# Multi-query attention on one core: the cube of a pair of units as one product, VectorE's units from the second on, planner settings by a table

## The chip, the core and the metric

The kernel runs on one core of a Trainium2 chip. Five engines of the core matter here. TensorE (PE in the profile; PEld is its weight load) multiplies matrices and writes to PSUM. ScalarE (ACT) evaluates the exponential. VectorE (DVE) and GpSimd (POOL) do elementwise work, GpSimd on SBUF alone. SyncE (SP) issues DMAs. Each engine runs its own instructions in order, and semaphores order them between engines. The metric is the device time of one execution in microseconds; smaller is better. The kernel before was timed three times: 744.91 us is the median, 744.78 and 746.61 the ends.

## The reference

Eight batches, 1,024 positions, 16 query heads of 64 numbers, one key and value head per batch:

```python
scores = np.matmul(q, k.transpose(0, 1, 3, 2)) / np.sqrt(head_dim)
weights = np.exp(scores - np.max(scores, axis=-1, keepdims=True))
weights = weights / np.sum(weights, axis=-1, keepdims=True)
attn_out = np.matmul(weights, v)
```

q, k, v and the output are fp32. The result is q's shape, (8, 1024, 16, 64).

## The kernel before

**Units.** Two heads are done together. For a pair of heads, a half of 512 queries and a tile of 128 keys the kernel makes one *unit*: `scores` (L279) multiplies the transposed keys by the transposed queries, one matmul of 512 columns for each head, and leaves 128 x 1,024 scores in PSUM. There are 8 batches x 8 head pairs x 2 halves x 8 key tiles = 1,024 units, 2,048 such matmuls. Three PSUM slots (`sc0` to `sc2`) hold units that wait to be exponentiated.

**Two ways to an exponential.** Most units go to ScalarE, which makes one ACTIVATE of 1,024 columns (`scalar_exp`, L292) into a tile `wt`. The others (called V units) go to VectorE. There `ve_bits` (L303) reads PSUM and writes the scores as int16 bits of an fp16 number. Two V units make a *pair* (`PAIR = 2`), and the next passes run on both at once, 2,048 columns: `ve_mantissa` (L316), `ve_power` (L326) and `ve_square` (L337). The last step is the *cube*, a product of the mantissa's number with its square. It is dealt between GpSimd (`ve_cube`, L345) and VectorE (`ve_rest`, L353): GpSimd takes some columns while VectorE does something that reads PSUM, VectorE takes what is left. Here a cube belongs to one unit and has 1,024 columns, since `cube_of` gives the columns of that unit alone. For a pair in the set `two`, `ve_shift` (L341) follows the square, and its units need two terms instead of three below.

**Values.** `value` (L420) multiplies the exponentials by the values: for each of 16 head pairs and halves of a batch (each is one `h` of the planner), 8 groups of 128 queries of one head, and in each group one matmul of 65 columns for each *term*. A ScalarE unit is one term, a V unit three (two in the set `two`): the power, the bits and the cube. All terms of a group must be there before its sum is complete; the order is first all units' own terms, then the powers, then the cubes. Seven groups fill a PSUM bank, which VectorE inverts and scales (`inverse` L370, `finish` L379) into `osb`; SyncE stores it.

**The order of the work** is written out ahead by `plan()`, a planner that runs on the host. It advances a modelled time of each engine with fixed costs (`T_MM`, `T_ACT`, `VE_COST`, `GP_COL` and others) and emits operations. At each step it decides whether TensorE does scores (`issue`) or values, which units go to VectorE (`wants`), what VectorE does next (`vector_step`), and how many columns GpSimd gets (`share`). A stretch of scores between two stretches of values is called a *round* here; it holds the scores of one or more units. What settles these choices are constants: `REST`, `DEFER`, `HOLD`, `VE_SLACK`, `RATE`, `SAFE` and others, the same for the whole run. `SAFE` (300 ns) is added to the time at which a value's input is ready in the model. `wants` allows V units from unit `NKT` (8) to unit `STEPS - V_END`. The queue of GpSimd also issues the loads of q and v, in `share`, right behind a cube.

**The start.** q of the first head pair arrives in fp32 (`qf`, two DMAs on ScalarE's queue). ScalarE casts the first half to fp16 (L868), VectorE the second (L875). TensorE transposes them (`first_q`, L232), and ScalarE or VectorE copies the result to `qt` (L245). Keys go the same way (`first_k`, L216 and L228). After unit 1 the second half of q is turned.

**The end.** The last `h` has its own 64 value matmuls (`last_values`), behind them reciprocals, a check of the sums and the last stores.

Of the kernel before, what the change touches and what calls it, by code (L numbers as in the profile page):

```python
# [26 lines left out]
TWO_N = 1  # L27
TWO_M = 16
LONE = 12
# [35 lines left out]
NEXT = {"bits": 0.0, "inverse": 0.0, "finish": 60.0}  # L65
MINC = 128
REST = 896
LATE = 0.0
EPS = 0.0
AWAY = 500.0  # L70
SLACK1 = -500.0
SOON = 0.0
FIRST = 90.0
DEFER = 12
HOLD = 1400.0
VE_SLACK = 1800.0
V_END = 16
RATE = 0.25
NEAR = 200.0
WAIT = 50.0  # L80
T_BITS = 1255.0
SAFE = 300.0
# [3 lines left out]
def attention_main(ctx, tc, q, k, v, out, flag):  # L86
# [46 lines left out]
        w3p.tile([P, PAIR, 3, 2, QCH], FP16, tag=f"w3_{N_W3 - 1}", name="qf")  # L133
        .rearrange("p n i h q -> p (n i h q)")[:, 0 : 2 * NKT * P]
# [33 lines left out]
    def load_q_first(p):  # L168
        x = wtp.tile([P, 2, QCH], FP16, tag=f"wt{N_WT - 1 - p}", name=f"q16_first{p}")
        q16[("first", p)] = x.rearrange("p h (c f) -> p (h c) f", f=P)  # L170
        src = q[0, :, 2 * p : 2 * p + 2, :].rearrange("(c p) h d -> p c (h d)", p=P)
        if p:
            nc.gpsimd.dma_start(out=q16[("first", p)], in_=src)
# [67 lines left out]
    def first_q_out(ps, p, cs, eng):  # L241
# [3 lines left out]
        eng(out=qt[0][:, p, at], in_=ps[:, at])  # L245
# [66 lines left out]
    def parts(u, n, i):  # L312
        return ve[u][:, 0:n, i]
# [37 lines left out]
    def ve_rest(u, lo):  # L351
        we, wu = cube_of(u)
        return nc.vector.tensor_tensor(  # L353
            out=wu[:, lo:], in0=we[:, lo:], in1=wu[:, lo:], op=ALU.mult
# [10 lines left out]
    def cube_of(u):  # L365
        return (ve[u, 0][:, i].rearrange("p h q -> p (h q)") for i in (1, 2))
# [124 lines left out]
    def plan():  # L491
# [5 lines left out]
        t_pe = t_ve = t_act = t_gp = t_now = 0.0  # L497
        mode = "v"
        u = 0
        free = [0.0] * 3  # L500
# [9 lines left out]
        members = {}  # L510
        lead = {}
# [32 lines left out]
        def cost(what, v):  # L544
            return VE_COST[what, 2] if (what, 2) in VE_COST and len(members[v]) == 2 else VE_COST[what]
# [5 lines left out]

        def share(s):
# [4 lines left out]
            v = next((v for v in left if left[v]), None)  # L557
            if v is not None:
# [3 lines left out]
                if n >= MINC:  # L562
                    lo = 2 * QCH - left[v]
                    emit(gs, "cube", v, lo, lo + n, gate)
                    left[v] -= n
                    lock = gs + GP_FIX + n * GP_COL
                    t_gp = lock + GP_TAIL
                    ready[v, 2] = max(ready.get((v, "g"), 0.0), t_gp)
                    ready[v, "g"] = ready.pop((v, 2))
# [6 lines left out]
        def passes(v):  # L576
            nonlocal half, made_2
            chain.extend([("mantissa", v), ("power", v), ("square", v)])
            half = None
            made_2 += 1  # L580
            if made_2 * TWO_N % TWO_M < TWO_N:
                chain.append(("shift", v))
                two.update(members[v])

        def vector_step(limit):

            nonlocal t_ve, t_gp, lock, behind, t_behind, early, last, half
            if half is not None and not todo and (flush or u - half > LONE or min(wt_used) == float("inf")):
# [3 lines left out]
            for x in [(r, "bits", v, 0) for v, r in todo] + evict:  # L592
                r, what = x[:2]
                s = max(t_ve, r, min(w3_used) if what == "bits" and half is None else 0.0)
                key = (max(s, t_ve + NEXT[what]), ORDER[what], x[2])
# [3 lines left out]
                best[1] <= t_ve + NEXT[best[2][1]]  # L599
                and (best[2][1] == "bits" or behind is not None or best[2][0] < t_ve - LATE or not chain)  # L600
            )
            if urgent and best[2][1] == "bits" and not any(left.values()):
                t = 0.0
                for what, v in chain:
                    t += cost(what, v)
                    if what == "square":
                        urgent = t > HOLD
                        break
            if not urgent and (
                chain or left and (flush or left[next(iter(left))] <= REST or u - next(iter(left)) > DEFER)  # L610
# [422 lines left out]
```

## Time and profile before

| | us |
|---|---|
| median of three runs | 744.91 |
| profiled execution | 745.27 |
| its span, first to last instruction | 743.3 |
| first score matmul starts | 6.33 |
| first ACTIVATE of line 292 starts | 6.98 |
| last ACTIVATE ends | 737.0 |
| the 64 last value matmuls start | 735.66 |

| engine | busy us | share of the span | instructions |
|---|---|---|---|
| TensorE matmul | 728.4 | 98% | 13,826 |
| TensorE weight load | 490.5 | 66% | 13,826 |
| ScalarE | 732.0 | 98% | 798 |
| VectorE | 713.0 | 96% | 1,139 |
| GpSimd | 362.4 | 49% | 306 |

Matmuls and ScalarE's operations overlap, so a busy share near 100% does not tell by itself which engine sets the pace; the starts of neighbouring instructions and the waits do. In a line of the timeline the columns are start, length, engine, line, operation, and in brackets the idle time before it with what ended it.

### The profile page before, as it was taken

Reading aid. Unit: us, or ns where it says so; the run is one execution under the profiler, and the core shown is the slowest. Engines: PE = TensorE matmul, PEld = TensorE weight load, DVE = VectorE, ACT = ScalarE, POOL = GpSimd, SP = SyncE. Lnnn points to the kernel's source line nnn. Section 1 sums busy time; section 2 is a strip of 40 time slices with the busy share of each in tenths; the row PEclk is TensorE's granted clock in tenths of the full one; section 3 lists DMA queues with packets and bytes.
Section 4 is the critical chain, followed back from the end, with each engine's and each line's share of the span. In section 5 each row is a group of like instructions: output and inputs, shape, how many; then the busy total and the mean of one; then the engine's idle time right before and its main releaser. Section 6 shows DMA issues by size and latency. Waiting matters only on the chain.

```text
span 743.3 us, 31083 instructions
## 1 busy us (share of the span) xinstructions
PE 728.4 (98%) x13826; PEld 490.5 (66%) x13826; DVE 713.0 (96%) x1139; ACT 732.0 (98%) x798; POOL 362.4 (49%) x306
## 2 busy tenths in 40 slices
PE   6999999999999999999999999999999999999997
PEld 3566666666666666666666666666666666666675
DVE  3999999999999999999999999999999999999994
ACT  7999999999999999999999999999999999999996
POOL 3555454554455554445454445554554544554540
PEclk9999999999999999999999999999999999999999
DMA  9986547665385654686358654365525765212112
GB/s 188 167 102 116 80 86 119 113 109 106 63 108 120 110 88 86 87 138 108 81 101 123 116 108 81 79 125 107 115 69 92 108 130 101 60 45 60 44 52 82
DMA packets 168921, 73.87 MB, mean 99 GB/s; under 512 B 94032, under 2 KB 161616, under 8 KB 168784
## 3 DMA queue, kind: packets, MB, share of 16 engines
q1 hardware_dynamic: 149152, 53.76, 34.8%
q0 software_dynamic: 18576, 17.57, 19.5%
q8 instruction: 109, 1.79, 1.0%
q10 hardware_dynamic: 1056, 0.52, 0.2%
q14 instruction: 28, 0.23, 0.1%
HBM read 37.75 MB, written 33.55 MB: 96 GB/s over the span
## 4 chain that ended last, share of the span: by engine, by line
PE 78%; ACT 15%; DVE 5%; issue 1%; DMA 0%; DVEq 0%; ACTq 0%
PE ot L420 46%; PE sc L279 32%; ACT wt L292 15%; DVE we L303 2%; DVE osb L379 1%; DVE we L337 1%; DMA knat<-in_k_dram 0%; DVE we L316 0%; DVE we L326 0%; DVE we L353 0%; PE kps L216 0%; DVE rec_all L370 0%; DVE ge L460 0%; DVE both L466 0%; DVE ok_all L470 0%
## 5 line engine op out<-in xcount | busy, mean ns | idle before, releaser
L292 ACT ACTIVATE wt<-sc 128x1024 f16<-128x1024 f32 x795 | 729.6, 1205 | 1.2 <-PE sc L279 1.1
L345 POOL TENSOR_TENSOR we<-we 128x832 f16<-128x832 f16 (+15 forms) x223 | 314.8, 1412 | 361.4 <-DVE we L337 225.6
L420 PE MATMUL ot<-vp,wt 128*128 128x65 f16 x6296 | 424.8, 194 | 0.2 <-ACT wt L292 0.2
L420 PE MATMUL ot<-vp,we 128*128 128x65 f16 x5384 | 416.7, 194 | 0.0
L420 PEld LDWEIGHTS <-wt 128*128 128x128 f16 x6296 | 314.5, 97 | 93.6 <-issue 93.2
L420 PEld LDWEIGHTS <-we 128*128 128x128 f16 x5384 | 310.7, 97 | 81.6 <-issue 79.8
L279 PE MATMUL sc<-qt,k2t 64*128 64x512 f16 x2048 | 341.4, 385 | 4.9 <-ACT wt L292 3.7
L303 DVE TENSOR_SCALAR we<-sc 128x1024 int16<-128x1024 f32 x229 | 278.4, 1216 | 8.0 <-PE sc L279 6.6
L279 PEld LDWEIGHTS <-k2t 64*128 64x128 f16 x2048 | 95.3, 93 | 66.0 <-issue 9.8
L337 DVE TENSOR_TENSOR we<-we 128x2048 f16<-128x2048 f16 (+1 forms) x115 | 138.2, 1202 | 0.0
L379 DVE TENSOR_TENSOR osb<-ot,rec_all 128x448 f32<-128x448 f32 x146 | 89.2, 611 | 0.4
L353 DVE TENSOR_TENSOR we<-we 128x512 f16<-128x512 f16 (+13 forms) x222 | 83.4, 377 | 0.0
L316 DVE TENSOR_SCALAR we<-we 128x2048 int16<-128x2048 int16 (+1 forms) x115 | 78.5, 682 | 0.3
L326 DVE TENSOR_SCALAR we<-we 128x2048 int16<-128x2048 int16 (+1 forms) x115 | 77.9, 678 | 0.0
L182 POOL DMA_DIRECT2D q<-in_q_dram x64 | 41.3, 648 | 2.0 <-DMA q_first<-in_q_dram 1.4
L370 DVE RECIPROCAL rec_all<-ot 128x7 f32<-128x7 f32 x146 | 28.5, 195 | 7.3 <-PE ot L420 7.3
L164 POOL DMA_DIRECT2D vp<-in_v_dram x8 | 7.3, 907 | 0.0
L216 PE MATMUL kps<-ident,k 128*64 128x128 f16 x16 | 1.3, 314 | 4.3 <-DVE k L207 4.2
L250 DVE TENSOR_SCALAR k16d<-knat 128x1024 f16<-128x1024 f32 x7 | 4.8, 682 | 0.0
L341 DVE TENSOR_SCALAR we<-we 128x2048 f16<-128x2048 f16 x7 | 4.7, 667 | 0.1
L245 DVE COPY qt<-qps 128x512 f16<-128x512 f16 (+1 forms) x2 | 1.1, 555 | 3.5 <-PE qps L232 3.5
L216 PEld LDWEIGHTS <-k 128*64 128x64 f16 x16 | 0.8, 159 | 4.6 <-DVE k L207 4.6
(31 smaller groups left out, 23.3 us busy)
## 6 DMA issues: line engine op xcount, KB each, us to landing
out_dram<-osb SPq DMA_DIRECT2D x109, 256.0 KB, 2.5
q<-in_q_dram POOLq DMA_DIRECT2D x56, 256.0 KB, 4.7
out_dram<-osb SPq DMA_DIRECT2D x38, 128.0 KB, 2.3
knat<-in_k_dram SPq DMA_DIRECT2D x7, 256.0 KB, 4.2
q<-in_q_dram POOLq DMA_DIRECT2D x8, 192.0 KB, 7.4
vp<-in_v_dram POOLq DMA_DIRECT2D x8, 128.0 KB, 6.4
qt<-q SPq DMA_TRANSPOSE x64, 4.9
qf<-in_q_dram ACTq DMA_DIRECT2D x2, 256.0 KB, 3.9
```

Source lines behind the costliest of these rows:

```text
L182: nc.gpsimd.dma_start(out=q16[(b, c)], in_=q[b, c * P : (c + 1) * P, h0:, :].rearrange("p h d -> p (h d)"),)
L279: nc.tensor.matmul(sc[u][:, hh, :], k2t[r : r + 64, j * P : (j + 1) * P], qt[b][r : r + 64, p % HP, c * QCH : (c + 1) * QCH], start=True, ...
L292: nc.scalar.activation(out=w, in_=sc.pop(u), func=EXP, scale=escale, bias=math.log(CS))
L303: return nc.vector.tensor_scalar(out=w3[:, 1].bitcast(I16), in0=sc.pop(u), scalar1=15.0 * 1024, scalar2=0.0, op0=ALU.add, op1=ALU.max,)
L316: return nc.vector.tensor_scalar(out=parts(u, n, 2).bitcast(I16), in0=parts(u, n, 1).bitcast(I16), scalar1=0x3FF, scalar2=0x3800, op0=ALU. ...
L326: return nc.vector.tensor_scalar(out=parts(u, n, 0).bitcast(I16), in0=parts(u, n, 1).bitcast(I16), scalar1=0x7C00, scalar2=0x0201, op0=ALU ...
L337: return nc.vector.tensor_tensor(out=m, in0=m, in1=m, op=ALU.mult)
L345: x = nc.gpsimd.tensor_tensor(out=wu[:, lo:hi], in0=we[:, lo:hi], in1=wu[:, lo:hi], op=ALU.mult)
L353: return nc.vector.tensor_tensor(out=wu[:, lo:], in0=we[:, lo:], in1=wu[:, lo:], op=ALU.mult)
L370: return nc.vector.reciprocal(out=rec_all[:, g0 : g0 + n], in_=o[:, 0:n, D])
L379: x = nc.vector.tensor_tensor(out=ob[:, i0 : i0 + n, :], in0=o[:, 0:n, 0:D], in1=rec.unsqueeze(2).broadcast_to([P, n, D]), op=ALU.mult,)
L420: nc.tensor.matmul(ots[g0][:, gg - g0, 0 : D + 1], w[:, hh, qb * P : (qb + 1) * P], kv[h // (HP * NCH)]["vp"][:, ci, u % NKT, 0 : D + 1], ...
```

## The change

- **Layout.** A pair's tile is `[P, 3, PAIR, 2, QCH]` instead of `[P, PAIR, 3, 2, QCH]`: each of the three parts (power, bits, mantissa) is now 2,048 neighbouring columns over both units.
- **Cube.** `cube_of` gives these 2,048 columns, so a cube and its rest belong to a pair and may cross from one unit to the other; `ve_rest` gets an upper bound. In the planner `left`, `squared` and `group` are kept by pair, and `cubed` notes for each unit when its last column is done.
- **V units** may begin with unit 1 (`V_START`) and reach to unit `STEPS - 12`. The planner counts VectorE and GpSimd as occupied for the first 2.5 and 2.6 us (`T_VE0`, `T_GP0`).
- **Settings by table.** 11 sets of 19 settings (`WAYS`), of which a letter of `TABLE` picks one for each stretch of 32 units. `safe`, which was 300 everywhere, is 0 in 10 of the 32 stretches, 150 in 7 and 300 in 15. `rate` is 1.0 (0.25 before), `rest` 640 to 1,536 (896), `defer` 16 or 20 (12). The choice of pairs with a shift is by a rule on VectorE's backlog (`two`) instead of every sixteenth pair.
- **Start.** q of the first head pair is transposed in fp32 straight from `qf` (`first_qf`); the two casts are gone. The first half goes through two score slots, two tiles each, copied by ScalarE and VectorE with 256 columns each. The second half of the keys is turned after unit 0, the second half of q after unit 1, and `prep_v` comes after unit 3.

Counted in the two built programs, in their order:

| | before | after |
|---|---|---|
| ACTIVATE of a unit | 795 | 792 |
| V units / pairs, singles among them | 229 / 115 | 232 / 116 |
| shift passes | 7 | 6 |
| value matmuls without the last 64 | 11,680 | 11,744 |
| rounds of one unit / two units | 311 / 349 | 279 / 365 |
| rounds of 3 / 6 / 9 units | 3 / 1 / 0 | 0 / 1 / 1 |
| GpSimd cubes, columns in all | 223, 138,688 | 149, 160,128 |
| VectorE rests, columns in all | 222, 95,808 | 113, 77,440 |
| loads of q, of v; stores; transposes by DMA | 64, 8; 147; 71 | the same |

```diff
-V_END = 16
-RATE = 0.25
-SAFE = 300.0
+V_END = 12
+V_START = 1
+Way = namedtuple(
+    "Way",
+    "slack wait near bits end late least rest defer hold rate safe away alone eps soon first lone two",
+)
+SPAN = 32
+TABLE = (
+    "feekajaddbabacdckibcabadbddfahag"
+)
+WAYS = (
+    Way(1500.0, 100.0, 200.0, 0.0, 60.0, 1500.0, 96, 640, 16, 350.0, 1.0, 300.0, 500.0, -500.0, 0.0, 0.0, 90.0, 16, -1.0),
+    Way(1800.0, 200.0, 2000.0, 0.0, 60.0, 2500.0, 96, 896, 16, 1400.0, 1.0, 0.0, 500.0, -200.0, 50.0, 0.0, 90.0, 8, -1.0),
...
+)
+T_VE0 = 2500.0
+T_GP0 = 2600.0
...
+    def first_qf(ps, cs):
+        for c in cs:
+            nc.tensor.matmul(
+                ps[:, (c - cs[0]) * P : (c - cs[0] + 1) * P],
+                qf[:, c, :],
+                ident,
+                is_transpose=True,
+                start=True,
+                stop=True,
+            )
...
-            ve[u] = w3p.tile([P, PAIR, 3, 2, QCH], FP16, tag=f"w3_{i}", name=f"we{p}_{c}_{j}")
-            ve[u, 0] = ve[u][:, 0]
-        else:
-            ve[u, 0] = ve[first][:, 1]
-        w3 = ve[u, 0]
+            ve[u] = w3p.tile([P, 3, PAIR, 2, QCH], FP16, tag=f"w3_{i}", name=f"we{p}_{c}_{j}")
+        w3 = ve[first][:, :, int(first != u)]
...
-        return (ve[u, 0][:, i].rearrange("p h q -> p (h q)") for i in (1, 2))
+        return (ve[u][:, i].rearrange("p n h q -> p (n h q)") for i in (1, 2))
...
+        def cubed(v, n, t):
+
+            lo = 2 * QCH * len(group[v]) - left[v]
+            left[v] -= n
+            for k, x in enumerate(group[v]):
+                if lo < (k + 1) * 2 * QCH <= lo + n:
+                    ready[x, 2] = t
...
-                NKT <= u < STEPS - V_END
+                V_START <= u < STEPS - V_END
...
-                and made_v < (u - NKT + 1) * RATE
+                and made_v < (u - V_START + 1) * way.rate
...
                 if r < float("inf"):
-                    r += SAFE
+                    r += way.safe
...
+        if u == 0:
+            first_k(kps, 1)
+            first_k_out(kps, 1)
+        if u == 3:
+            prep_v(0)
         if u == 1:
-            first_q(turned[0], 0, range(NKT // 2, NKT))
-            first_q_out(turned[0], 0, range(NKT // 2, NKT), nc.vector.tensor_copy)
+            turned[0] = bank("qps0")
+            first_qf(turned[0], range(NKT // 2, NKT))
+            first_q_out(turned[0], 0, range(NKT // 2, NKT), nc.vector.tensor_copy, NKT // 2)
...
-        nc.scalar.copy(out=q0[:, 0 : NKT // 2, :], in_=qf[:, 0 : NKT // 2, :])
         first_k(kps, 0)
-        first_q(turned[0], 0, lo)
-        first_q_out(turned[0], 0, lo, nc.scalar.copy)
+        ps = [scp.tile([P, 2, QCH], FP32, tag=f"sc{i + 1}", name=f"qps0_{i}")[:, 0] for i in range(2)]
+        for i in range(2):
+            first_qf(ps[i], range(2 * i, 2 * i + 2))
+        first_q_out(ps[0], 0, range(0, 2), nc.scalar.copy, 0)
         first_k_out(kps, 0)
-        first_k(kps, 1)
-        first_k_out(kps, 1)
-        nc.vector.tensor_copy(out=q0[:, NKT // 2 :, :], in_=qf[:, NKT // 2 :, :])
-        prep_v(0)
+        first_q_out(ps[1], 0, range(2, 4), nc.vector.tensor_copy, 2)
```

More of the change, by code (lines that the diff above doesn't have):

```diff
@@ L556, in share @@
                 return
-            v = next((v for v in left if left[v]), None)
+            v = next(iter(left), None)
             if v is not None:
@@ L605, in vector_step @@
                     t += cost(what, v)
-                    if what == "square":
-                        urgent = t > HOLD
+                    if what == ("shift" if v in two else "square"):
+                        urgent = t > way.hold
                         break
             if not urgent and (
-                chain or left and (flush or left[next(iter(left))] <= REST or u - next(iter(left)) > DEFER)
+                chain or left and (flush or left[next(iter(left))] <= way.rest or u - next(iter(left)) > way.defer)
             ):
```

133 lines of the change are left out of this document (66 added, 67 removed).

## The prediction

> **What bounds the kernel now.** I read the table of windows first, then TensorE's waits, then the timeline around one round, then the chain and the groups. Windows (busy us of PE, PEld, DVE, ACT and POOL, then granted clock and DMA):
>
> ```profile
> 6.33:28.00 21.67, 18.18 (x198) 9.03 (x197) 14.57 (x21) 20.65 (x23) 5.71 (x12) 0.92 1.19 180
> 100.00:200.00 100.00, 100.00 (x1903) 67.73 (x1902) 99.19 (x156) 100.00 (x110) 52.34 (x43) 1.00 0.57 97
> 200.00:225.00 25.00, 24.20 (x472) 16.16 (x471) 24.90 (x40) 25.00 (x28) 11.27 (x10) 1.00 0.79 116
> 350.00:600.00 250.00, 249.70 (x4780) 168.30 (x4776) 247.34 (x394) 250.00 (x274) 127.11 (x103) 1.00 0.55 102
> ```
>
> TensorE, ScalarE and VectorE are all full, GpSimd half. The chain of work that ended last and TensorE's waits tell them apart:
>
> ```profile
> PE 78%; ACT 15%; DVE 5%; issue 1%; DMA 0%; DVEq 0%; ACTq 0%
> ...
> PE sc L279 <- ACT wt L292: 3.7, 10, 0.5
> PE sc L279 <- DVE we L303: 1.0, 3, 0.6
> ```
>
> In 743 us TensorE waits under 5 us for a score slot, and hardly for a value's input. So its own work is the bound, once it is fed. What that work costs is read in the timeline of weight loads:
>
> ```profile
> 404.17 0.13 PEld L420 LDWEIGHTS <-we 128*128 128x128 f16 x2
> 404.35 0.10 PEld L279 LDWEIGHTS <-k2t 64*128 64x128 f16 x2
> 404.68 0.15 PEld L420 LDWEIGHTS <-wt 128*128 128x128 f16 x3 [0.23 <-issue]
> ...
> 730.26 0.10 PEld L420 LDWEIGHTS <-wt 128*128 128x128 f16 x1
> 730.40 0.32 PEld L279 LDWEIGHTS <-k2t 64*128 64x128 f16 x4
> 730.95 0.10 PEld L420 LDWEIGHTS <-wt 128*128 128x128 f16 x1 [0.23 <-issue]
> ...
> 733.01 0.97 PEld L420 LDWEIGHTS <-wt 128*128 128x128 f16 x30
> ```
>
> Values follow each other at (0.97 - 0.10) / 29 = 0.030 us; over all stretches of the timeline the mean is 0.0295. From the last value before a round of one unit to the first behind it is 0.48 us (404.20 to 404.68), the median of all such 0.473; for two units 0.69 (730.26 to 730.95), the median 0.690. Less the value's own step, a round of one unit costs 0.4435 and one of two 0.6605: the second unit in a round adds only 0.217. With the counts of the program, before is 11,680 x 0.0295 = 344.6, plus 311 x 0.4435 = 137.9, plus 349 x 0.6605 = 230.5, plus the four longer rounds 4.1: **717.1 us of work**. It begins at 6.33, and the last 64 values begin at 735.66, so TensorE was idle 735.66 - 6.33 - 717.1 = 12.2 us. Summing the same prices along the timeline puts 9.3 us of this before 28 us and 2.9 after it. Check: 6.33 + 717.1 + 12.2 + 7.64 (tail to 743.3) + 1.97 (743.3 to 745.27) = 745.24.
>
> **Part by part: TensorE's work.** 64 more values: +1.9. 32 fewer rounds of one unit, -14.2; 16 more of two, +10.6; three of three (0.8775 each) go, -2.6; the round of 9, +2.2. After: 346.4 + 123.7 + 241.1 + 3.7 = 714.9, **-2.2 us**. All of it is on the path. ScalarE has 3 units fewer at 0.904 (the commonest distance of two ACTIVATE starts), -2.7, no separate gain.
>
> **The start.** The chain to the first score is here:
>
> ```profile
> 4.21 0.64 PE L216 MATMUL kps<-ident,k 128*64 128x128 f16 x8 [4.21 <-DVE k L207]
> 4.38 0.62 ACT L868 CAST q_first<-qf 128x512 f16<-128x512 f32 x1 [1.20 <-DMA qf<-in_q_dram]
> 5.05 0.61 PE L232 MATMUL qps<-ident,q_first 128*128 128x128 f16 x4 [0.20 <-ACT q_first L868]
> 5.70 0.58 ACT L245 COPY qt<-qps 128x512 f16<-128x512 f16 x1 [0.70 <-PE qps L232]
> 6.33 1.04 PE L279 MATMUL sc<-qt,k2t 64*128 64x512 f16 x4
> 8.54 0.29 DVE L267 TENSOR_SCALAR vp<-vp 128x512 f16<-128x512 f16 x1 [1.36 <-DMA vp<-in_v_dram]
> ```
>
> The ACT cast goes (0.62), and the copy is halved between two engines. The four transposes are fp32 now, and the trace has none of that. Lower bound: the fp16 row, 0.61 for four. Upper bound: the score matmul of four times the columns, 0.385 each in the groups, 1.54 for four. They start at 4.65, behind the keys' issue. VectorE's copy of the keys (4.89 to 5.31) and its 256 columns of q (0.25) follow: first score at 5.6 to 6.6. I take 6.1, the middle, for neither row is near: -0.2. [...]
>
> What follows decides more. Unit 1 goes to VectorE, but its bits stand behind `prep_v`, which waits for v's DMA (8.54 before), so they start at 8.8; if q's second half is late, 10.3. Behind them up to the first pair's rest stand five bits (1.13), a copy of q (0.65), two each of mantissa and power (0.60) and square (1.14), one rest (0.6): 11.6 us. The cube is whole at 20.4 to 22, and TensorE can't pass the first group of half 0 before that. By then its work is 18 units and 12 values, 6.2 us, so its idle time is 8.2 to 9.4. From there it has a half's 96 values at hand, and the next pair's cube is about 5.3 us of VectorE work behind, 26 us. I take 9.3 as before; bounds 8.3 and 11.3. The second unit of ScalarE comes behind eight key transposes, score 1 and four fp32 ones, 0.3 to 1.5 us after it is free: inside the same idle time, since TensorE lacks the cube anyway.
>
> **VectorE and GpSimd.** Groups and VectorE's timeline:
>
> ```profile
> L353 DVE TENSOR_TENSOR we<-we 128x1024 f16<-128x1024 f16 x14 | 9.5, 678 | 0.0
> L353 DVE TENSOR_TENSOR we<-we 128x192 f16<-128x192 f16 x36 | 8.8, 245 | 0.0
> ...
> L345 POOL TENSOR_TENSOR we<-we 128x512 f16<-128x512 f16 x65 | 75.3, 1159 | 162.2 <-DVE we L337 100.0 <-PE sc L279 35.6 <-PE ot L420 19.5
> L345 POOL TENSOR_TENSOR we<-we 128x1024 f16<-128x1024 f16 x4 | 8.8, 2207 | 13.7 <-DVE we L337 6.7 <-DVE rec_all L370 3.5 <-DVE we L341 3.4
> ```
>
> A rest costs 0.52 ns a column (433 ns for 832 columns) and some 0.065 us besides, its overlap with the next taken off: 64.2 before, 113 x 0.065 + 77,440 x 0.00052 = 47.6 after, -16.6. Three bits, one pair's passes and one shift less add 5.1: VectorE is 11.5 us lighter. GpSimd gains 21,440 columns at about 2.05 ns and loses 74 starts of 0.11: some +36 of 315 us, under its 381 idle. Loads of q and v stand behind its cubes, now one in 5 us instead of 3.3; their transposes come 20 units (14 us) later, and landing took 4.7, so that wait stays hidden, with SyncE's stores behind it.
>
> VectorE is not the bound, so its relief pays only where it was late: idle 2.9 after 28 us, the largest piece in 200 to 225, where three check operations (214.84 to 216.43) delay bits and TensorE waits 0.55 and 0.25 for them. I take 0.5 of the 2.9, 0 and 2.9 being the ends of this gain.
>
> A long cube can also cost VectorE: in the timeline a cube ends in the median 0.06 us after the next pass on SBUF has started, and rests of 512 columns beside cubes lasted 427 ns where the line through 192 and 1,024 columns gives 412. I leave it at that, since there are fewer cubes. [...]
>
> **Sum:** 6.1 + 714.9 + 9.3 + 2.4 + 7.64 + 1.97 = 742.3 against 745.27. The profiled execution lies 0.36 above the median of the runs, so 742.0 beside 744.91.
>
> **Rivals.** (1) The gain is eaten. (1a) At the start: fp32 transposes at the upper end and a late first cube, idle 11.3 instead of 9.3: 744.5. For it: nothing feeds TensorE but that one cube. Against: before idles as long. [...] (2) Slower: TensorE meets cubes that aren't done. `safe` is 0 in 10 of 32 stretches, 40 halves of units. A wait for GpSimd in a value was 0.9 us in three times, 0.3 each. At 0.3 a half it is 12 us, 754; at half of that 748. It equals the gain at 0.07 us a half, and is slower by 0.3% at 0.13. Against: only three such waits before. (3) The lighter VectorE takes away all 2.9 of the later idle time and the start its 1 us: 738.6 to 740.
>
> **Numbers.** Forecast 0.50, its own range 740.6 to 743.6; (1a) 0.14, (1b) 0.08; (2) 0.16; (3) 0.12. 0.3% of 744.91 is 2.2 us, about what a measurement can tell from no change: 742.7 and 747.1. Faster: four fifths of the forecast, all of (3), a little of (1) and (2): 0.56. Slower: half of (2): 0.08. Same: 0.36. The range of 739.6 to 746.2 leaves out the lower half of (3) and the upper half of (2) and little else.
>
> **What would show it.** Right: first score at 5.6 to 6.6, 20 to 22 us for the first group's end, TensorE idle 9 to 10 by 28 us and under 3 after, 792 ACTIVATEs back to back. [...]

## The result and the profile after

The changed kernel takes 747.9 us, the median of 22 runs (746.9 to 748.6). The kernel before, run beside it as often, takes 746.11 (744.78 to 747.5). The ratio is 1.0026, with a 95% interval of 1.0019 to 1.0033: **slower by a quarter of a per cent**. That is inside the 0.3% called "no change" ahead, but the interval excludes 1, the sign is opposite to the forecast, and 747.9 lies above the range of 739.6 to 746.2. The 744.91 shown ahead was the median of three runs; of the 22, nine lie under 745.0 and eleven over 746.2. The median of such a set jumps, so kernels are compared below by their ratios to runs of the kernel before made beside them.

The profiled execution took 747.03 and has a span of 745.3 (before: 745.27 and 743.3). With the prices of the prediction (0.0295 a value, 0.4435 a round of one unit, 0.6605 a round of two) summed along each trace, the span falls into five parts. What is left over at such a price counts as idle, so a matmul at half clock leaves its excess there.

| us | before | after | difference |
|---|---|---|---|
| first score starts | 6.33 | 6.40 | +0.1 |
| TensorE's work by prices | 716.7 | 714.5 | -2.2 |
| TensorE idle up to 28 us | 9.3 | 12.5 | +3.2 |
| TensorE idle later | 3.3 | 4.1 | +0.8 |
| tail behind the last 64 values' start | 7.64 | 7.76 | +0.1 |
| span | 743.3 | 745.3 | +2.0 |

The loss is in the first 28 us. The table of windows of the changed kernel (busy us of PE, PEld, DVE, ACT, POOL, then granted clock, DMA share and GB/s) shows it in its first row:

```profile
6.40:28.00 21.60, 16.27 (x136) 7.25 (x138) 16.91 (x21) 17.78 (x19) 9.45 (x13) 0.84 1.20 189
100.00:200.00 100.00, 99.77 (x1932) 66.94 (x1932) 98.84 (x141) 99.75 (x110) 51.28 (x28) 1.00 0.48 98
200.00:225.00 25.00, 25.00 (x492) 17.01 (x488) 24.57 (x37) 25.00 (x29) 14.85 (x8) 1.00 0.63 119
350.00:600.00 250.00, 249.70 (x4826) 170.33 (x4826) 245.93 (x355) 249.66 (x273) 136.31 (x74) 1.00 0.55 101
```

In mid-run TensorE is as full as before, and does more matmuls in the same time (4,826 against 4,780 in the last row, whose counterpart stands in the prediction). In the first row it does 136 where the kernel before does 198, ScalarE is busy 17.78 us instead of 20.65, and the granted clock is 0.84 instead of 0.92. Two things happen there. The first is in the timeline behind the first score (start, length, engine, line, operation):

```profile
4.77 1.12 PE L249 MATMUL qps<-ident,qf 128*128 128x128 f32 x4
...
6.40 0.61 PE L296 MATMUL sc<-qt,k2t 64*128 64x512 f16 x2 [0.52 <-DVE qt L262]
...
6.94 0.64 PE L222 MATMUL kps<-ident,k 128*64 128x128 f16 x8
7.05 1.02 ACT L309 ACTIVATE wt<-sc 128x1024 f16<-128x1024 f32 x1 [1.19 <-PE sc L296]
7.51 0.61 PE L296 MATMUL sc<-qt,k2t 64*128 64x512 f16 x2
...
8.05 1.11 PE L249 MATMUL qps<-ident,qf 128*128 128x128 f32 x4
...
9.10 1.04 PE L296 MATMUL sc<-qt,k2t 64*128 64x512 f16 x4
...
9.74 2.85 ACT L309 ACTIVATE wt<-sc 128x1024 f16<-128x1024 f32 x3 [1.67 <-PE sc L296]
...
10.02 1.21 DVE L317 TENSOR_SCALAR we<-sc 128x1024 int16<-128x1024 f32 x1
```

Between the first unit and ScalarE's second stand eight key transposes, the score of unit 1 (VectorE's) and four fp32 transposes of q. ScalarE is free at 8.07 and starts at 9.74; before, its second ACTIVATE started at 7.90. VectorE's first bits start at 10.02, though their score was done by 8.12 (7.51 + 0.61): VectorE's queue has other work ahead of them, shown at late_turns below.

The second is the granted clock. The same view in smaller windows, of the kernel before and then of the changed one:

```profile
14.00:20.00 6.00, 5.23 (x84) 3.14 (x81) 4.72 (x6) 6.00 (x8) 0.00 (x0) 1.00 1.33 174
20.00:24.00 4.00, 2.97 (x18) 1.07 (x17) 4.00 (x7) 4.00 (x5) 2.65 (x3) 0.92 0.87 155
24.00:28.00 4.00, 4.00 (x61) 2.55 (x60) 3.77 (x5) 3.63 (x5) 1.45 (x2) 0.65 1.04 180
```

```profile
14.00:20.00 6.00, 3.50 (x25) 1.20 (x22) 5.97 (x8) 5.51 (x7) 1.90 (x2) 1.00 1.14 197
20.00:24.00 4.00, 2.70 (x19) 0.80 (x17) 3.88 (x5) 3.62 (x5) 3.62 (x3) 0.57 1.07 128
24.00:28.00 4.00, 4.00 (x58) 2.49 (x57) 2.88 (x4) 3.36 (x4) 2.34 (x2) 0.58 1.22 237
```

From 14 to 20 us TensorE does 25 matmuls instead of 84, since with VectorE's units in the first half it has hardly a group to finish without a cube. Then the clock falls to 0.50 for 6.83 us (20.57 to 27.39), against 3.41 us before (23.35 to 26.77). Just then the first cube becomes whole, and TensorE has values to do. GpSimd's last piece and VectorE's rest of that cube, in the timeline:

```profile
20.36 2.11 POOL L359 TENSOR_TENSOR we<-we 128x544 f16<-128x544 f16 x1 [0.58 <-DVE we L340]
...
22.45 0.66 DVE L367 TENSOR_TENSOR we<-we 128x992 f16<-128x992 f16 x1
```

It is whole at 23.11 (22.45 + 0.66), where the prediction said 20.4 to 22.

### The profile page after: what moved, and what is told of

Read it like the earlier page. It is cut to its first block, busy times and chain, and to the rows that moved or that the text cites. A ratio compares the mean times of both kernels' runs of the same rounds, so it can differ in the third digit from the quotient of the medians.

```text
span 745.3 us, 31135 instructions
## 1 busy us (share of the span) xinstructions
PE 729.1 (98%) x13890; PEld 490.6 (66%) x13890; DVE 712.2 (96%) x1035; ACT 729.7 (98%) x794; POOL 399.4 (54%) x232
## 4 chain that ended last, share of the span: by engine, by line
PE 87%; DVE 9%; ACT 2%; issue 1%; DMA 1%; DVEq 0%
PE ot L434 51%; PE sc L296 35%; DVE we L317 4%; ACT wt L309 2%; DVE we L351 1%; DVE osb L393 1%; DVE we L340 1%; DVE we L330 1%; DMA out_dram<-osb 0%; DMA knat<-in_k_dram 0%; DVE we L367 0%; PE qps L249 0%; PE last L457 0%; DVE rec_all L384 0%; PE kps L222 0%
## 5 line engine op out<-in xcount | busy, mean ns | idle before, releaser
L359 POOL TENSOR_TENSOR we<-we 128x1472 f16<-128x1472 f16 (+19 forms) x149 | 348.7, 2341 | 327.7 <-DVE we L351 188.8
L434 PE MATMUL ot<-vp,we 128*128 128x65 f16 x5472 | 421.1, 194 | 0.0
L434 PEld LDWEIGHTS <-we 128*128 128x128 f16 x5472 | 317.3, 98 | 92.4 <-issue 91.2
L317 DVE TENSOR_SCALAR we<-sc 128x1024 int16<-128x1024 f32 x232 | 282.1, 1216 | 12.5 <-PE sc L296 11.5
L351 DVE TENSOR_TENSOR we<-we 128x2048 f16<-128x2048 f16 x116 | 139.3, 1201 | 0.0
L296 PEld LDWEIGHTS <-k2t 64*128 64x128 f16 x2048 | 93.4, 93 | 65.1 <-issue 13.2
L330 DVE TENSOR_SCALAR we<-we 128x2048 int16<-128x2048 int16 x116 | 81.9, 706 | 1.5
L340 DVE TENSOR_SCALAR we<-we 128x2048 int16<-128x2048 int16 x116 | 79.5, 685 | 0.0
L367 DVE TENSOR_TENSOR we<-we 128x544 f16<-128x544 f16 (+22 forms) x113 | 57.8, 511 | 0.0
L188 POOL DMA_DIRECT2D q<-in_q_dram x64 | 43.4, 681 | 2.0 <-DMA vp<-in_v_dram 1.1
```

The costliest lines, as they stand in the source:

```text
L188: nc.gpsimd.dma_start(out=q16[(b, c)], in_=q[b, c * P : (c + 1) * P, h0:, :].rearrange("p h d -> p (h d)"),)
L296: nc.tensor.matmul(sc[u][:, hh, :], k2t[r : r + 64, j * P : (j + 1) * P], qt[b][r : r + 64, p % HP, c * QCH : (c + 1) * QCH], start=True, ...
L317: return nc.vector.tensor_scalar(out=w3[:, 1].bitcast(I16), in0=sc.pop(u), scalar1=15.0 * 1024, scalar2=0.0, op0=ALU.add, op1=ALU.max,)
L330: return nc.vector.tensor_scalar(out=parts(u, n, 2).bitcast(I16), in0=parts(u, n, 1).bitcast(I16), scalar1=0x3FF, scalar2=0x3800, op0=ALU. ...
L340: return nc.vector.tensor_scalar(out=parts(u, n, 0).bitcast(I16), in0=parts(u, n, 1).bitcast(I16), scalar1=0x7C00, scalar2=0x0201, op0=ALU ...
L351: return nc.vector.tensor_tensor(out=m, in0=m, in1=m, op=ALU.mult)
```

## The experiments

Three theories for the 3.2 us at the start. **A, turns:** the transposes of keys and q between the first scores ("turns") delay the second ACTIVATE and VectorE's first bits, and with them everything behind. **B, clock:** the scarce work lets the granted clock fall, and the values run at half speed. **C, early units of VectorE:** with VectorE's units from unit 1 on, TensorE lacks work until the first cube. Rivals in mid-run: long cubes, late cubes. One table for all runs; times and ratios beside it. "Half clock" is the length of the stretches at 0.50 before 40 us. The columns of work, idle time, half clock and ACTIVATEs come from one profiled execution of each kernel, the ratios from all its runs.

| kernel | TensorE's work | idle to 28 us | idle later | half clock | 1st, 2nd ACTIVATE | median, us | ratio to before |
|---|---|---|---|---|---|---|---|
| before | 716.7 | 9.3 | 3.3 | 3.41 | 6.98, 7.90 | | 1 |
| after | 714.5 | 12.5 | 4.1 | 6.83 | 7.05, 9.74 | 747.9 | 1.0026 [1.0019, 1.0033] |
| late_turns | 714.5 | 11.3 | 4.1 | 6.83 | 7.10, 8.02 | 745.99 | 1.0006 [0.9996, 1.0017] |
| old_start | 714.5 | 12.4 | 3.9 | 10.24 | 7.02, 8.54 | 746.36 | 1.0003 [0.9993, 1.0012] |
| after_warm | 719.9 | 7.4 | 4.0 | 0 | 7.13, 10.60 | 747.31 | 1.0017 [1.0008, 1.0027] |
| after_warm2 | 716.5 | 9.5 | 4.5 | 0 | 7.14, 9.84 | 746.19 | 1.0005 [0.9996, 1.0014] |
| late_turns_warm | 716.5 | 8.1 | 4.2 | 0 | 7.14, 8.06 | 744.56 | 0.9980 [0.9971, 0.9989] |
| before_warm | 723.0 | 4.8 | 3.4 | 0 | 6.99, 7.91 | 747.03 | 1.0017 [1.0007, 1.0026] |
| before_warm2 | 720.0 | 6.9 | 3.6 | 3.41 | 6.99, 7.91 | 746.39 | 1.0009 [1.0000, 1.0018] |
| before_v1 | 716.0 | 11.7 | 3.8 | 10.24 | 6.98, 8.49 | 748.46 | 1.0038 [1.0025, 1.0051] |
| pair_alone | 716.1 | 11.3 | 4.0 | 6.83 | 7.02, 7.95 | 747.0 | 1.0013 [1.0003, 1.0022] |
| late_v | 713.5 | 8.0 | 7.0 | 0 | 6.90, 7.82 | 745.64 | 0.9989 [0.9979, 0.9998] |
| late_v_warm | 715.9 | 8.2 | 6.8 | 0 | 7.30, 8.22 | 747.01 | 1.0013 [1.0003, 1.0023] |

In the kernels with "warm" in the name some scores are issued twice with the same result; the second issue is part of the column of work and puts 0.217 us a unit into it.

### The turns: late_turns and old_start

late_turns turns the second half of the keys after unit 2 (not 0) and the second half of q after unit 4 (not 1). `prep_v` stays behind unit 3, so it now comes ahead of q's second half; all else is as in the changed kernel:

```diff
-        if u == 0:
+        if u == 2:
             first_k(kps, 1)
             first_k_out(kps, 1)
         if u == 3:
             prep_v(0)
-        if u == 1:
+        if u == 4:
             turned[0] = bank("qps0")
             first_qf(turned[0], range(NKT // 2, NKT))
```

> The changed kernel with its fp32 transposes, but the second half of the keys is turned after unit 2 (not 0), the second half of q after unit 4 (not 1), so that scores 0, 1 and 2 follow each other. Theory A: as with the old start, second ACTIVATE 0.9 us after the first, idle by 28 us 10.7 to 11.7, span 743.5 to 744.5. If fp32 as such were the cost (first score at 6.40 instead of 6.33), nothing is gained beyond 0.1 us. Theory C: idle over 11.5.

Measured: the second ACTIVATE starts at 8.02 instead of 9.74, and the ratio falls from 1.0026 to 1.0006, some 1.5 us of 746. The timeline of late_turns shows the first ACTIVATEs without a gap:

```profile
6.45 1.46 PE L296 MATMUL sc<-qt,k2t 64*128 64x512 f16 x6 [0.52 <-DVE qt L262]
...
7.10 3.90 ACT L309 ACTIVATE wt<-sc 128x1024 f16<-128x1024 f32 x4 [1.19 <-PE sc L296]
...
7.84 0.64 PE L222 MATMUL kps<-ident,k 128*64 128x128 f16 x8
```

VectorE's queue changes too. In the changed kernel its first bits stand behind its copy of q's second half, which waits for the fp32 transposes, and behind `prep_v`:

```profile
9.20 0.69 DVE L262 CAST qt<-qps 128x512 f16<-128x512 f32 x1 [1.15 <-PE qps L249]
9.81 0.29 DVE L284 TENSOR_SCALAR vp<-vp 128x512 f16<-128x512 f16 x1
```

In late_turns that copy comes behind them:

```profile
9.15 1.20 DVE L317 TENSOR_SCALAR we<-sc 128x1024 int16<-128x1024 f32 x1
...
10.79 0.69 DVE L262 CAST qt<-qps 128x512 f16<-128x512 f32 x1 [0.44 <-PE qps L249]
```

The bits start 0.87 us earlier, the first cube is whole at 22.25 (23.11 in the changed kernel), 0.86 us earlier, the idle time to 28 us is 1.2 us less, and the half clock is as long as it was. So A is a cause, for about half of the 3.2 us, and it needs no change of the clock: the mean granted clock of all runs is 0.9935 here and 0.9940 in the changed kernel. How much of it goes through the second ACTIVATE and how much through VectorE's queue, this run doesn't part.

old_start brings the whole start of the kernel before back, with the two casts and fp16 transposes:

```diff
-        if u == 0:
-            first_k(kps, 1)
-            first_k_out(kps, 1)
-        if u == 3:
-            prep_v(0)
         if u == 1:
-            turned[0] = bank("qps0")
-            first_qf(turned[0], range(NKT // 2, NKT))
-            first_q_out(turned[0], 0, range(NKT // 2, NKT), nc.vector.tensor_copy, NKT // 2)
+            first_q(turned[0], 0, range(NKT // 2, NKT))
+            first_q_out(turned[0], 0, range(NKT // 2, NKT), nc.vector.tensor_copy)
...
+        nc.scalar.copy(out=q0[:, 0 : NKT // 2, :], in_=qf[:, 0 : NKT // 2, :])
         first_k(kps, 0)
...
+        first_q(turned[0], 0, lo)
+        first_q_out(turned[0], 0, lo, nc.scalar.copy)
         first_k_out(kps, 0)
-        first_q_out(ps[1], 0, range(2, 4), nc.vector.tensor_copy, 2)
+        first_k(kps, 1)
+        first_k_out(kps, 1)
+        nc.vector.tensor_copy(out=q0[:, NKT // 2 :, :], in_=qf[:, NKT // 2 :, :])
+        prep_v(0)
```

> The changed kernel with the start of the kernel before: q of the first head pair is cast to fp16 and transposed as before, both halves of the keys are turned ahead of the first score; the order of everything from the first score on is that of the changed kernel. Three theories on the 12.5 us that TensorE is idle by 28 us in the changed kernel (9.3 before). Theory A, the order at the start: four fp32 transposes and eight key transposes stand between the first scores, and ScalarE's second ACTIVATE came 1.8 us late. Then the second ACTIVATE follows the first at once, the first pair's cube is whole 1 to 1.8 us earlier (21.2 to 22 us instead of 23.0), idle falls to 10.7 to 11.5, and the span to 743.5 to 744.3. Theory B, the granted clock: it was 0.50 for 6.8 us (20.6 to 27.4) instead of 3.4, and idle falls only as far as that stretch is shorter. Theory C, V units from unit 1 make TensorE wait for a cube, whatever the order: idle stays over 11.5 and the span over 744.6.

Measured: ratio 1.0003. The first score starts at 6.37 against 6.40, so the fp32 transposes neither win nor lose at that point. The second ACTIVATE starts at 8.54, 1.2 us earlier than in the changed kernel. VectorE's first bits start at 8.87, earlier than in late_turns, but its second bits wait 1.09 us for a score, and the cube is whole at 22.54: both paths of A count. The idle time to 28 us is 12.4 all the same in the profiled execution (746.71, above its median), where the half clock is 10.24 us long. A and B are mixed in this run, and the next ones part them.

### The clock: after_warm, before_warm, and later after_warm2, before_warm2

The edit gives TensorE work while it waits: the scores of a stretch of units are issued twice, into the same slot.

```diff
-        for hh in range(2):
+        for hh in (0, 1, 0, 1) if 1 <= u < 26 else (0, 1):
```

In before_warm the bounds are 1 and 30, in after_warm2 9 and 18, in before_warm2 10 and 25.

> The changed kernel with the two score matmuls of units 1 to 25 issued twice into the same tile (the second overwrites the first): 25 x 0.217 = 5.4 us more work for TensorE, all in the time in which it is idle. Theory B, that TensorE's idle time at the start lowers the granted clock: the stretch at 0.50 (20.6 to 27.4 us) goes or halves, values of that stretch come at 0.030 instead of 0.055 us, and the span falls by 1 to 2 us in spite of the added work. Theories A and C: no gain; 0 to 3 us slower, for the added work lies ahead of scores that ScalarE waits for.

> The kernel before with the score matmuls of units 1 to 29 issued twice, 29 x 0.217 = 6.3 us more work while TensorE is idle (9.3 us by 28 us). Theory B: the 3.4 us at a clock of 0.50 (23.4 to 26.8) go, 0.5 to 1.5 us faster, and its runs, which spread from 744.8 to 747.5, lie closer together. Without B: the same or up to 3 us slower.

Measured: both keep the clock at 1.00 until the last 1.4 and 0.7 us. after_warm goes from 1.0026 to 1.0017, before_warm from 1 to 1.0017. The added scores are 5.4 and 6.3 us of TensorE's work, much of it outside the time in which it waits. By 28 us, 24 of the 25 and 26 of the 29 units are done, 5.2 and 5.6 us of added work. With the idle time that makes 12.6 and 10.4 us, no less than the idle time alone was (12.5 and 9.3). The clock was kept, and its price paid in full. That tells nothing yet of what the clock costs, so the stretch was cut to the units that lie in the wait for the first cube.

> The changed kernel as it is, with the score matmuls of units 9 to 17 issued twice and nothing else. It splits what late turns and the second scores gave together (744.56 against 747.9). Theory B alone takes away the 6.8 us at half clock: 1 to 1.7 us faster than the changed kernel, 746.2 to 746.9, idle time by 28 us with the added work counted as work 9 to 9.7; the rest, 1.2 to 2 us, belongs to the order of the turns (A).

> The kernel before with the score matmuls of units 10 to 24 issued twice (14 to 26 us), 15 x 0.217 = 3.3 us more work; units 1 to 9, whose scores ScalarE waits for, are left alone, unlike in the first try. Theory B: the runs at 746.3 and 747.5 of the kernel before go, all within 1 us, median 744 to 745, that is 0.5 to 1.5 us below the median before. If the second state of its runs has another cause than the clock at the start: the spread stays 2 us or more.

Measured: after_warm2 adds 2.0 us, has no half clock, and its ratio is 1.0005, some 1.6 us better than the changed kernel (746.19 against 747.9). The windows of after_warm2:

```profile
20.00:24.00 4.00, 2.91 (x22) 1.03 (x20) 4.00 (x6) 4.00 (x5) 3.39 (x4) 1.00 0.91 121
24.00:28.00 4.00, 3.98 (x79) 2.75 (x79) 3.96 (x5) 4.00 (x6) 2.54 (x2) 1.00 1.22 145
```

Between 24 and 28 us TensorE does 79 matmuls where the changed kernel does 58 at a clock of 0.58. The first cube isn't earlier, it is whole at 23.83, 0.72 us later than in the changed kernel, so the gain lies behind it, where the values come. So B is a cause too; the repeated scores that keep the clock give about the other half of the 3.2 us.

In before_warm2 a stretch of 3.41 us at half clock remains, only earlier (12.45 to 15.86), and the kernel is no faster (1.0009). Its runs spread over 2 us (745.84 to 747.88) as those of the kernel before do.

The mean granted clock of each run is on record too, and by it the clock's own price stays open. In the kernel before the time goes with it: of its 89 runs beside the experiments, 23 have 0.997 or more, and 22 of these took 744.65 to 744.95 (the other 745.92), while the 66 at 0.994 to 0.996 took 744.96 to 747.56. Elsewhere it doesn't. Three of the 22 runs of the changed kernel have 0.999, which leaves no room for a stretch of 3.41 us, and they took 747.44 to 747.55, only some 0.4 under its median; two at 0.990 took 746.90 and 746.98. Five runs of before_warm2 at 0.999 or 1.000 took 745.84 to 747.31. So the 1.6 us are what the repeated scores gave. That all of it comes through the clock isn't shown, and neither is what spreads the runs.

### VectorE's units from the second on: before_v1 and late_v

before_v1 is the kernel before with early units. With them goes the limit of one V unit in four, for the whole run, and the planner counts VectorE and GpSimd as occupied for the first 2.5 and 2.6 us; nothing else of the change is in it:

```diff
-        t_pe = t_ve = t_act = t_gp = t_now = 0.0
+        t_pe = t_act = t_now = 0.0
+        t_ve, t_gp = 2500.0, 2600.0
...
-                NKT <= u < STEPS - V_END
+                1 <= u < STEPS - V_END
...
-                and made_v < (u - NKT + 1) * RATE
+                and made_v < u * 1.0
```

> The kernel before with V units allowed from unit 1 (not 8), VectorE counted as occupied for the first 2.5 us, and no limit of one unit in four; nothing else of the change. V units are 1 and 6, then 9 and 12, and so on; TensorE's work by the prices of the prediction is 716.0 us (716.7 before). Theory C, an early V unit makes TensorE wait for its cube: the first pair's cube is whole at about 21 us, TensorE's idle time by 28 us rises from 9.3 to 11 or 12, and the kernel is 1 to 2 us slower. If C is wrong: idle 9 to 9.6 and the same or 0.5 us faster.

Measured: ratio 1.0038, slower by some 2.8 us. The idle time to 28 us is 11.7 instead of 9.3, and the half clock 10.24 us long. Its timeline shows TensorE waiting for the bits of early units, with few values to do in between:

```profile
14.26 0.61 PE L279 MATMUL sc<-qt,k2t 64*128 64x512 f16 x4 [1.30 <-DVE we L303]
...
16.11 1.04 PE L279 MATMUL sc<-qt,k2t 64*128 64x512 f16 x4 [0.76 <-DVE we L303]
```

So early units, with these two settings, cost more than the whole change does (1.9 us by its ratio). This is C, and B comes with it: TensorE has less to do before the first cube, and the clock falls for longer. Its idle time after 28 us rose only from 3.3 to 3.8, so little of the loss is in mid-run.

late_v is the changed kernel with the old start, VectorE's units from unit 9 on, and a table chosen anew for that:

```diff
-V_START = 1
+V_START = 9
...
-    "feekajaddbabacdckibcabadbddfahag"
+    "kkcjbcadkqcqqbhcqcqbbqaibedhqqbh"
```

Seven more sets of settings belong to its table.

> The changed kernel (cubes of pairs, settings by a table, V units up to unit 1011) with the start of the kernel before and V units from unit 9 on, with another table of settings fitted to that. TensorE's work is 713.5 us by the prices (716.7 before, 714.5 changed). Theory C: idle by 28 us is 9 to 9.8 as before, so the gain of the work shows: span 740.3 to 742, 1.5 to 3 us faster than the kernel before. If the pairs' cubes and the table cost TensorE waits in mid-run, idle after 28 us is above 4.5 (3.3 before, 4.1 changed) and the kernel is no faster than before.

Measured: ratio 0.9989, against 1.0003 of old_start, from which it differs by the early units and the table. The idle time to 28 us is 8.0, the lowest of the kernels without repeated scores, with no half clock in the profiled execution. That execution is the shortest of its 11 runs, though (744.19; the median is 745.64, and mean clocks go down to 0.995). The idle time later is 7.0 instead of 3.9, and why was not found; the largest single piece, 0.84 us at 363.8, is a round of two units in which a score waits 0.52 us for ScalarE. The windows of late_v show the start with work:

```profile
14.00:20.00 6.00, 5.10 (x82) 3.21 (x82) 5.45 (x6) 6.00 (x8) 0.58 (x1) 1.00 1.26 161
20.00:24.00 4.00, 3.13 (x32) 1.39 (x31) 3.93 (x8) 4.00 (x5) 4.00 (x3) 1.00 0.81 182
```

82 matmuls between 14 and 20 us, nearly the 84 of the kernel before.

### The cube of a pair alone: pair_alone

The layout and the product of 2,048 columns, with the old start, units from 8 on, one set of settings, and a shift for every sixteenth pair:

```diff
-V_END = 12
-V_START = 1
+V_END = 16
+V_START = 8
...
-SPAN = 32
-TABLE = (
-    "feekajaddbabacdckibcabadbddfahag"
+SPAN = 1024
+TABLE = "a"
+WAYS = (
+    Way(1800.0, 50.0, 200.0, 0.0, 60.0, 0.0, 128, 512, 16, 1400.0, 0.25, 300.0, 500.0, -500.0, 0.0, 0.0, 90.0, 12, -1.0),
 )
...
```

Its `rest` is 512 and its `defer` 16 (896 and 12 before), so it isn't the pure layout.

> Of the change only the layout and the cube of a pair as one product: start, first V unit, V_END and the constants are those of the kernel before, save REST 512 and DEFER 16 for a left part of 2,048 columns instead of 1,024. Work 716.1 us (716.7). Theories A and C: start as before, idle by 28 us 9 to 9.8, span within 0.8 us of 743.3. [...]

Measured: ratio 1.0013. The loss is at the start here too: 11.3 us idle to 28, and half clock from 24.47 to 31.29. Its timeline shows what is late there, GpSimd's first piece:

```profile
21.71 2.91 POOL L347 TENSOR_TENSOR we<-we 128x1440 f16<-128x1440 f16 x1 [12.26 <-DVE we L339]
```

It ends at 24.62; in the kernel before, the first piece has 736 columns and ends at 21.89 (20.31 + 1.58). After 40 us its idle time is 2.7, not more than the 3.3 of the kernel before: long cubes cost nothing that shows in mid-run here. late_v has long cubes as well and 7.0 us of later idle time, so for its plan that stays open.

### Both remedies: late_turns_warm and late_v_warm

late_turns_warm has the edit of late_turns and scores issued twice for units 9 to 17; late_v_warm is late_v with that for units 9 to 19.

> The kernel with late turns (second halves of keys and of q turned after units 2 and 4) and the score matmuls of units 9 to 17 issued twice: 9 x 0.217 = 2.0 us more work, all within the round in which TensorE waits for the first cube. Theory B: the stretch at a clock of 0.50 (19.0 to 25.9 us with late turns) goes, the halves behind the first cube run at 0.030 a value, 0.5 to 1.5 us faster than late turns (span 744.1). If the added matmuls delay ScalarE's input by as much as the clock gives: within 0.4 us of it.

> The kernel with V units from unit 9 on and the start of before, and the score matmuls of units 9 to 19 issued twice, 11 x 0.217 = 2.4 us more work in the stretch in which TensorE has little to do (13 to 23 us). Its profile without them fell on an execution with no stretch at half clock (744.19), its other runs reach 746.2. Theory B: the runs lie within 1 us of each other, at 743.9 to 744.9, median 1 us lower than without. If the added matmuls delay scores: median no lower than 745.6.

Measured: late_turns_warm takes 744.56, ratio 0.9980 [0.9971, 0.9989]. It beats the changed kernel by 3.3 us and the kernel before by 0.2%. Some weight loads of the values right behind the first cube, and then the same ones in the changed kernel:

```profile
22.64 0.16 PEld L434 LDWEIGHTS <-wt 128*128 128x128 f16 x3
22.73 0.10 PEld L434 LDWEIGHTS <-we 128*128 128x128 f16 x1
22.77 0.12 PEld L434 LDWEIGHTS <-wt 128*128 128x128 f16 x2
22.82 0.13 PEld L434 LDWEIGHTS <-we 128*128 128x128 f16 x2
```

```profile
23.70 0.24 PEld L434 LDWEIGHTS <-wt 128*128 128x128 f16 x3
23.87 0.13 PEld L434 LDWEIGHTS <-we 128*128 128x128 f16 x1
23.93 0.19 PEld L434 LDWEIGHTS <-wt 128*128 128x128 f16 x2
24.04 0.19 PEld L434 LDWEIGHTS <-we 128*128 128x128 f16 x2
```

Six values take 0.18 us in the one, at a granted clock of 1.00, and 0.34 in the other, at 0.50: 0.030 and 0.057 each, and the values begin 1.05 us earlier (22.49 against 23.54). The two remedies add up within the intervals: -1.5 by the turns (1.0026 to 1.0006), -1.6 by the clock (1.0026 to 1.0005), -3.4 by both (to 0.9980).

late_v_warm is slower than late_v, 1.0013 against 0.9989. late_v had no half clock to cure in its profiled execution, and 2.4 us of scores were added. Its first score came 0.4 us later as well (6.65 against 6.25). Why the added scores found so little idle time wasn't settled.

## Why the prediction was wrong

**The sum.** It said 742.3 for a profiled execution that took 747.03. Of the 4.7 us, 3.2 are in the start, 1.3 in the later idle time (below), 0.3 in the first score and 0.1 in the tail; the time outside the span was 0.2 less. Another 1.2 us of the distance from 742.0 to 747.9 is no step of the sum: the profiled execution of the kernel before lay 0.36 above the median of its three runs, that of the changed one lies 0.87 under the median of its 22.

**TensorE's work: right.** -2.2 us was said, and the same prices along the trace give -2.2. The prices held: from the last value before a round to the first behind it, TensorE's matmul starts are 0.448 us apart in the median in both kernels for one unit, 0.663 and 0.664 for two. The sum along the trace puts 0.4 us less into work and more into idle time than the counts did, in both kernels. 792 ACTIVATEs are there. GpSimd went from 315 to 348.7 us of cubes (some 351 was said).

**The first score: the middle of bounds, a little late.** 6.40, between 5.6 and 6.6. Four fp32 transposes took 1.12 us, between 0.61 and 1.54, and 1.12 / 0.61 = 1.8 times the four fp16 ones of the kernel before. The 0.2 us that the start was to gain are not there: the late part is VectorE's copy (5.92 to 6.34, 0.42 where 0.25 was said), behind the fourth transpose.

**The start: the step that failed.** "I take 9.3 as before; bounds 8.3 and 11.3" was measured at 12.5, outside its own bounds. Three parts of that step were wrong.

- The second ACTIVATE was put "inside the same idle time, since TensorE lacks the cube anyway", at 0.3 to 1.5 us. It came 1.67 us late, and late_turns, in which neither it nor VectorE's first bits are late, is 1.5 us shorter. The cube hangs on both: the turns of q delay the first bits through VectorE's queue, a late score delays the second, these delay the passes behind them, and the cube was whole at 23.11 instead of 20.4 to 22. An engine that waits for the end of a chain gives no cover to a delay at the chain's beginning.
- The first bits started at 10.02, within the 8.8 to 10.3 that were said. The chain from them to the whole cube was put at 11.6 us, VectorE's busy time alone; it took 13.1 (10.02 to 23.11). Its timeline has the operations that were listed, and two waits that were not:

```profile
10.02 1.21 DVE L317 TENSOR_SCALAR we<-sc 128x1024 int16<-128x1024 f32 x1
12.16 1.23 DVE L317 TENSOR_SCALAR we<-sc 128x1024 int16<-128x1024 f32 x1 [0.94 <-PE sc L296]
13.63 0.69 DVE L262 COPY qt<-qps 128x1024 f16<-128x1024 f16 x1 [0.24 <-PE qps L238]
```

With 1.2 us for these, 10.02 + 11.6 becomes 22.8; the last 0.3 us is the passes themselves, 11.9 instead of 11.6. The second bits wait for a score that TensorE issues only when ScalarE, late itself, has given a slot free (at 11.73, behind a wait of 0.52 us for it).
- The granted clock was not in the sum at all. It was in view: the window row of the kernel before, 6.33 to 28, had 0.92. The prediction read the busy columns only, while a start with fewer matmuls was to follow. The remedy for the clock alone, the repeated scores of after_warm2, is worth 1.6 us.

Rival 1a, "a late first cube, idle 11.3 instead of 9.3", 744.5 us, was the mechanism in its second half, and its size too small: 11.3 was an upper bound for the cube alone, with the clock as before. Its first half, fp32 transposes at the upper end, did not happen.

**The later idle time: the wrong sign.** Ahead, 0.5 of 2.9 us was to go; on the same base it rose from 3.3 to 4.1. VectorE's relief was not there to pay. It was put at 11.5 us, and all its operations together went only from 713.0 to 712.2. The rests did what was said: with overlaps taken off along the trace they took 17.2 us less (16.6 said). Against that stand, counted the same way, 4.2 us more of bits, 6.2 of mantissa passes, 3.6 of `finish`, 1.6 of powers and 1.1 of squares, where the units and passes that are added were to make 5.1 together. About half of the mantissa's 6.2 is the order: a mantissa pass right behind bits overlaps with nothing and takes 0.694 us or more, one behind a rest 0.610 in the kernel before, and 44 stand behind bits now instead of 10. The mantissa passes also became a little longer, in the changed kernel and in the one before:

```profile
L330 DVE TENSOR_SCALAR we<-we 128x2048 int16<-128x2048 int16 x116 | 81.9, 706 | 1.5
```

```profile
L316 DVE TENSOR_SCALAR we<-we 128x2048 int16<-128x2048 int16 x114 | 78.1, 685 | 0.3
```

Waits of the changed kernel (engine and tile that wait, who is waited for: us in all, times, longest):

```profile
DVE we L317 <- PE sc L296: 11.5, 26, 1.5
...
PE sc L296 <- ACT wt L309: 3.9, 9, 0.7
...
PE sc L296 <- DVE we L317: 1.8, 3, 1.1
...
PEld L434 <- POOL we L359: 0.7, 2, 0.4
```

VectorE also waits 11.5 us for scores now (6.6 before). What of the later idle time comes from its missing relief, and what from the table, no run parts.

**The other rivals.** Rival 2 (cubes that aren't done, where `safe` is 0) is refuted by the last row above: values wait for GpSimd 0.7 us in two times, 0.9 in three before. Rival 1b was that cubes outlast their cover, VectorE's pass on PSUM beside which they run, at 0.2 us a cube, which was the author's estimate and which no run shows. Its outcome is there, VectorE's relief gone and the later idle time at 4.1 us, but not by that price: of the mantissa passes right behind bits, the 37 that start beside a running cube last 715 ns in the mean and the 7 others 694, 0.02 us more, a tenth of it. pair_alone, with 91 cubes of 1,280 columns and more (80 in the changed kernel) and 2.7 us idle after 40 us, speaks against it as the cause of the idle time. Rival 3 did not happen.

## What to carry to other kernels

Cost the first tens of microseconds as a chain of their own, from the first transfer to the first complete sum, and count a delay at its head in full even where the bound engine is idle: it waits for that chain. Read the clock column of a stretch before its work is taken away, since TensorE, which lost work there, ran at a granted clock of 0.50 when the work came (20.57 to 27.39 us in the changed kernel, where values took 0.057 us each instead of 0.030). Work issued twice to keep the clock paid where it filled the wait for one long thing that is known in advance: it gave 1.6 us in the changed kernel (after_warm2), and cost 1.3 us in the kernel before (before_warm), where it fell on time in use. A relief counted from fewer operations is there only if the order that follows keeps the overlaps of the rest: VectorE's 11.5 us came to 0.7.

## What the hardware showed that was not expected

The granted clock has two values in these traces, 1.00 and 0.50, and the stretches at 0.50 before 40 us last 3.41, 6.83 or 10.24 us: one, two or three times 3.41. In the changed kernel it fell at 20.57 us. The waits of score matmuls ahead of the fall, in its timeline:

```profile
16.11 0.61 PE L296 MATMUL sc<-qt,k2t 64*128 64x512 f16 x4 [1.10 <-DVE we L317]
...
17.83 0.39 PE L296 MATMUL sc<-qt,k2t 64*128 64x512 f16 x2 [0.56 <-ACT wt L309]
18.74 0.63 PE L296 MATMUL sc<-qt,k2t 64*128 64x512 f16 x4 [0.52 <-ACT wt L309]
19.66 0.39 PE L296 MATMUL sc<-qt,k2t 64*128 64x512 f16 x2 [0.29 <-ACT wt L309]
```

The longest is 1.10 us, and TensorE was busy 3.50 of the 6 us from 14 to 20. In after_warm2 it was busy 5.25 of them, and the clock stayed at 1.00. A limit can't be read from the busy share, though: in the 3.41 us ahead of its fall TensorE was busy 2.35 us in the kernel before (19.94 to 23.35), and in after_warm2 it was busy 2.32 us in such a stretch (19.19 to 22.60) and the clock did not fall. What sets the fall was not found.

GpSimd's product takes longer where it starts beside VectorE's square: 608 columns took 2,028 ns in the mean of ten, and 1,352 in the mean of five in the kernel before. The groups by shape, of the changed kernel and of the one before:

```profile
L359 POOL TENSOR_TENSOR we<-we 128x608 f16<-128x608 f16 x10 | 20.3, 2028 | 7.0 <-DVE we L340 6.5 <-DVE we L317 0.4
```

```profile
L345 POOL TENSOR_TENSOR we<-we 128x608 f16<-128x608 f16 x5 | 6.8, 1352 | 0.0
```

The timeline of VectorE and that of GpSimd show one of the ten:

```profile
25.70 1.22 DVE L351 TENSOR_TENSOR we<-we 128x2048 f16<-128x2048 f16 x1
...
25.86 2.25 POOL L359 TENSOR_TENSOR we<-we 128x608 f16<-128x608 f16 x1 [1.66 <-DVE we L340]
```

Seven of the ten start 0.16 us behind a square, with some 1.05 us of it to go, and take 2.23 to 2.26 us. One starts with 0.63 us of a square to go and takes 1.83. The two that start beside other passes take 1.36, as all five in the kernel before do. So the excess is about what is left of the square, less 0.16 us. No run varies this start alone.
